# Two-layer encoder trunk on one core: the last down-projection block of the second tokens in two 256-column pieces at the mixers, and the first tokens' transposes in two parts

## The chip, the cores and the metric

The kernel runs on one core of one Trainium2 chip. The metric is device time in microseconds of one execution; lower is better. A core has five engines with a queue each: TensorE (PE in the rows; its weight loads are PEld), VectorE (DVE), ScalarE (ACT), GpSimd (POOL) and SyncE (SP, which issues DMAs). TensorE's results land in the banks of PSUM, from which VectorE and ScalarE read them.

## The reference

An encoder of two layers over 256 tokens of 1024 features, all in float32. Each layer is an FFN, a mixer and a second FFN, each with a residual, and a last norm follows:

```python
x = x + FFN_RES * swiglu(rms_norm(x, ffn1_norm[l]), ffn1_w_gate[l], ffn1_w_up[l], ffn1_w_down[l])
h = rms_norm(x, mix_norm[l])
proj = h @ w_in[l]
...
y = jnp.concatenate([rms_norm(y_rec, lru_out_norm[l]), rms_norm(y_att, attn_out_norm[l])], axis=-1)
x = x + y @ w_out[l]
x = x + FFN_RES * swiglu(rms_norm(x, ffn2_norm[l]), ffn2_w_gate[l], ffn2_w_up[l], ffn2_w_down[l])
```

with `rms_norm(x, g) = x * rsqrt(mean(x*x) + eps) * g`, `swiglu = (silu(x @ w_gate) * (x @ w_up)) @ w_down`, and D_FF = 2816. The mixer has a recurrent group of eight blocks (convolution, gates, a scan in both directions) and a windowed attention with eight heads.

## The kernel before, in words

**Precision.** Every float32 matmul is made of three: the weights are split into `wh` and `wl`, the activations into `xh` and `xl` (or `hh` and `hl`), and `wh*xh + wl*xh + wh*xl` is summed in PSUM. ScalarE writes the high part as a copy with rounding (L303 for weights, L540 for x), VectorE the low part as a difference (L304, L542).

**Stages.** There are six: FFN, mixer, FFN, twice. x stays in SBUF as two tiles of 128 tokens x 1024, "first tokens" (t = 0) and "second tokens" (t = 1). An FFN's hidden width is 22 blocks of 128 (NM = 22). Its body computes gate and up of a block and, some blocks later, adds the block's share of the down projection to four accumulators in PSUM: two banks `ps_a` for the first tokens, two banks `ps_b` for the second, 512 columns each. The last four blocks (TAIL = 4) are left to `tail`, which the boundary calls.

**The boundary** (`boundary`, L588 to L623) joins a stage to the next. It finishes the down projection for the first tokens (`tail(0, 0)`), adds each half to x (`evac`, L792), takes the sums of squares on ScalarE (`squares`, L510), rstd (a sum on VectorE, L497, a power on POOL, L500), and the norm in four pieces of 256 columns (L517). Meanwhile TensorE does most of the second tokens' tail: `tail(1, 1)`, four blocks for the first half of the columns and three (CUT = 3) for the second. Then come eight transposes of the first tokens (`transposes(0)`, L535, into `ps_a`), the last block of the second half (`tail(1, 2)`: three matmuls of 128x512, L581 to L583), `head(0)`, eight transposes of the second tokens (into `ps_b`) and `head(1)`. In a mixer, `head` is `natural` (L543 to L552): 24 matmuls of 128x256, k = 0 to 7 three times (`xh*wh`, `xh*wl`, `xl*wh`), with the weights `w_w` for k 0 to 3 and `w_i` for k 4 to 7. In an FFN it is 24 matmuls of 128x512 (L697). Boundaries 1 and 4 lead into mixers (`gi % 3 == 1`), 2, 3 and 5 into FFNs.

**Buffers.** `xn_p` has one buffer: the tile `xn` (128x1024) holds the squares, which nobody reads, then the norm, and goes from the first tokens to the second and into the next stage. Banks `ps_g` and `ps_c` are taken in turn by `bank("gc")`.

**What sets the order.** TensorE, SP and POOL run in the order of the program. ScalarE and VectorE are ordered at build time by a scheduler, which takes what is inside `front()` first; the order is then fixed, and each engine works its queue off in that order. `prefetch` splits weights ahead (L303 and L304), at a boundary behind the instructions in `state["behind"]`.

Of the kernel before, what the change touches and what calls it, by code (L numbers as in the profile page):

```python
# [32 lines left out]
TAIL = 4  # L33
# [8 lines left out]
MAHEAD = 5  # L42
# [13 lines left out]
CUT = 3  # L56
# [11 lines left out]
def encoder_kernel(  # L68
# [313 lines left out]
    def setup_early():  # L382
        idle = ep_p.tile([128, T], F32R, tag="th", name="idle")
        dve.memset(idle.bitcast(F32), 0.0)
        pi = bank("b")

        def keep_warm(n):
            for _ in range(n):
                pe.matmul(pi[:, 0:T], idle[:, 0:128], idle, start=True, stop=True)

        dve.memset(half_t, -0.5)
        dve.memset(ones_t, 1.0)
        load_x(0)
        rows8 = xn_p.tile([128, DM], F32, tag="xn", name="rows8")[0:KD, 0:128]
        nc.scalar.dma_start(out=rows8, in_=ffn1_norm[0].rearrange("(k c) -> k c", c=128))
        nc.scalar.dma_start(out=eye_t, in_=eye)
        ps = bank("b")
        keep_warm(WARM)
        pe.transpose(ps[:, 0:KD], rows8, eye_t[0:KD, 0:KD])
        keep_warm(WARM2)  # L400
        dve.tensor_copy(out=gcol, in_=ps[:, 0:KD])
# [7 lines left out]

    def first_norm(t):  # L410
        r = rstd_of(ss_t[t], 2)
        xn = xn_t[t] = xn_p.tile([128, DM], F32, tag="xn", name="xn")
        for c in range(0, DM, 256):
            dve.tensor_scalar(xn[:, c:c + 256], xt[t][:, c:c + 256], r, None, ALU.mult)

    def first_transposes(t):
        if t == 0:
            new_x()
        for hf in range(2):
            ps = bank("ab"[t])  # L420
            for j in range(4):
                k = hf * 4 + j
                xT[t, k] = ps[:, j * 128:(j + 1) * 128]
                pe.transpose(xT[t, k], xn_t[t][:, k * 128:(k + 1) * 128], eye_t)

    def first_split(lo, t, k):
        ts_, g = slice(t * 128, (t + 1) * 128), gcol[:, k:k + 1]
# [74 lines left out]

    ss_t = {}

    def squares(t, hf):
        if hf == 0:
            ss_t[t] = st_p.tile([128, 2], F32, tag="ss", name="ss")
            xn_t[t] = xn_p.tile([128, DM], F32, tag="xn", name="xn")
        sl = slice(hf * 512, hf * 512 + 512)
        return act.activation(out=xn_t[t][:, sl], in_=xt[t][:, sl], func=AF.Square,  # L510
                              scale=1.0 / math.sqrt(DM), accum_out=ss_t[t][:, hf:hf + 1])

    def norm(t, gi):
        r = rstd_of(ss_t[t], 2)
        for c in range(0, DM, 256):
            sl = slice(c, c + 256)
            ins = dve.scalar_tensor_tensor(out=xn_t[t][:, sl], in0=xt[t][:, sl], scalar=r, in1=gain_t[gi][:, sl],  # L517
                                           op0=ALU.mult, op1=ALU.mult)
        return ins

# [1 line left out]
        cur["x"] = x_p.tile([128, 2, KD, T], F32R, tag="xhl", name="xhl")  # L522
        cur["h"], cur["l"] = cur["x"][:, 0], cur["x"][:, 1]

    def transposes(t):
        if t == 0:
            new_x()
        xn = xn_t.pop(t)
        ts_ = slice(t * 128, (t + 1) * 128)
        parts = []  # L530
        for hf in range(2):
            ps = bank("ab"[t])
            for j in range(4):
                k = hf * 4 + j
                pe.transpose(ps[:, j * 128:(j + 1) * 128], xn[:, k * 128:(k + 1) * 128], eye_t)  # L535
# [49 lines left out]
    def front():  # L585
        return tc.high_priority(offset=FRONT)

    def boundary(tail, evac, gi, head, ahead):  # L588
        prefetch(ahead)
        state["cap"] = ahead  # L590
        state["ahead"] = AHEAD
        tail(0, 0)
        with front():
            for hf in range(2):
                evac(0, hf)
                squares(0, hf)
            norm(0, gi)
        tail(1, 1)
        with front():
            evac(1, 0)  # L600
            transposes(0)
            squares(1, 0)
        tail(1, 2)
        with front():
            evac(1, 1)
            i1 = squares(1, 1)
            i2 = norm(1, gi)
        prefetch(ahead)
# [73 lines left out]
    def ffn(st, acc_done):  # L682
# [78 lines left out]
        def dn(m, t, hfs, fin):  # L761
            if t not in acc:
                acc[t] = [bank("ab"[t]) for _ in range(2)]
            hh, hl = hh_t[m]
            for hf in hfs:
                end = NM - TAIL if st == (DEPTH - 1, 2) and (t, hf) == (1, 1) else NM
                stream(acc[t], hh, hl, W(st, "d", m), t, (hf,), m == 0, m == end - 1)
            if fin:
                done((st, "d", m))
                del hh_t[m]  # L770

        def tail(t, part):
# [50 lines left out]

        if st == (DEPTH - 1, 2):
            tail, evac = dn_cols, acc
        return head if st != (0, 0) else first_head, body, tail, evac

    def mix(l):
        st = (l, 1)
# [157 lines left out]
        def att_pt(i):  # L987
            pr = stat.pop(i)
            if "pt" not in late:
                late["pt"] = xn_p.tile([128, 2, 512], F32, tag="xn", name="pt")  # L990
            for e in range(2):
                ps = bank("b")
                for kb in range(2):
                    for b in range(2):
                        c = kb * T + b * 128
                        pe.transpose(ps[:, c:c + 128], pr[:, e, b, kb * 128:(kb + 1) * 128], eye_t)
                pt = late["pt"][:, e, :]
                act.activation(out=pt, in_=ps, func=AF.Copy)

        def att_pv(i):  # L1000
            if not po:
                for b in range(2):
                    po[b] = bank("a")
            for e in range(2):
                h = i + 4 * e
                pt = late["pt"][:, e, :]
# [13 lines left out]
        def att_norm(t):  # L1020
            if "o" not in late:
                late["o"] = mix_p.tile([128, 2, 512], F32, tag="ql", name="o")
            o = late["o"][:, t, :]
            dve.tensor_tensor(out=o.rearrange("p (h d) -> p h d", h=NH),
                              in0=po[t].rearrange("p (h d) -> p h d", h=NH),
                              in1=nm_t[:, :, t:t + 1].to_broadcast([128, NH, 64]), op=ALU.mult)
            ss = st_p.tile([128, 2], F32, tag="ss", name="ss")
            act.activation(out=late["pt"][:, t, :], in_=o, func=AF.Square, scale=1.0 / math.sqrt(LW), accum_out=ss[:, 0:1])
            ra[t] = rstd_of(ss, 1)

        def o_split(t):
# [93 lines left out]
                if n == "D":  # L1125
                    load_gain(3 * l + 2)

        return head, body, tail, evac

    engines = mybir.EngineType  # L1130
    with tc.manual_schedule(engines={engines.PE, engines.SP, engines.Pool}):
# [16 lines left out]
        state["behind"] = []  # L1148
        load_gain(1)
        for s in range(3 * DEPTH):  # L1150
            _, body, tail, evac = stages[s]
            body()
            n = s + 1
            if n == 3 * DEPTH:
# [52 lines left out]
```

## Time and profile before

| | us |
|---|---|
| median of 3 runs | 940.01 (939.6 to 940.08) |
| profiled execution | 940.3 |
| its span | 938.5 |
| TensorE busy | 925.9 (99% of the span) |
| VectorE busy | 696.5 (74%) |
| ScalarE busy | 544.7 (58%) |
| POOL busy | 37.0 (4%) |

The profiled execution is one run with the profiler on; its span goes from the first instruction to the last, and 1.8 us lie around it. Matmuls overlap: a row's duration is from start to the end of its result, and the next matmul starts before that end. So the time that a matmul takes on TensorE is read from the distance of two starts. "x8" in a row is a run of eight instructions, with the time from the first's start to the last's end. "[0.44 <-DVE xn L517]" is idle time before the row and what ended it.

### The profile page before, as it was taken

What the parts mean: (1) busy time and instruction counts of PE and PEld (TensorE: products, weight loads), DVE (VectorE), ACT (ScalarE), POOL (GpSimd) and SP (SyncE); (2) the same over time, 40 slices, a digit from 0 to 9 for tenths busy, and PEclk for the clock granted to TensorE, in tenths of its full rate; (3) what the DMA queues carried; (4) which work ended last, traced back from release to release, by engine and by line L of the source; (5) the groups of instructions that cost most, each with busy time, mean ns of one, the idle gap of its engine ahead of it and who ended that gap; (6) DMA issues with size and microseconds to landing.
All of it is one profiled execution on the core that took longest, in us unless ns stands there. A gap on an engine that the chain in (4) does not pass through costs nothing.

```text
span 938.5 us, 13682 instructions
## 1 busy us (share of the span) xinstructions
PE 925.9 (99%) x5288; PEld 804.8 (86%) x5288; DVE 696.5 (74%) x1212; ACT 544.7 (58%) x1006; POOL 37.0 (4%) x58
## 2 busy tenths in 40 slices
PE   8999999999999999999999999999999999999997
PEld 7888888889988888888888888888999888888885
DVE  6877666759998866666688666666799887666663
ACT  7755555547865655555466555554687565555542
POOL 4100000000010000000030000000000100000000
PEclk9999999999999999999999999999999999999999
DMA  8966955614255866565557565655162566665521
GB/s 279 304 211 200 326 192 183 228 64 154 91 157 179 262 197 191 179 192 196 175 174 252 181 186 198 199 179 179 49 223 68 180 233 203 197 196 182 184 86 45
DMA packets 124993, 172.54 MB, mean 184 GB/s; under 512 B 3920, under 2 KB 108792, under 8 KB 124928
## 3 DMA queue, kind: packets, MB, share of 16 engines
q1 hardware_dynamic: 122192, 166.21, 54.7%
q0 software_dynamic: 2288, 4.87, 1.6%
q8 instruction: 41, 0.67, 0.3%
q10 hardware_dynamic: 448, 0.59, 0.2%
q14 instruction: 24, 0.20, 0.1%
HBM read 170.59 MB, written 3.16 MB: 185 GB/s over the span
## 4 chain that ended last, share of the span: by engine, by line
PE 92%; ACT 2%; DVE 2%; DMA 1%; issue 1%; POOL 0%; POOLq 0%; DVEq 0%; ACTq 0%
PE ps_g L572 16%; PE ps_c L572 15%; PE ps_g L571 7%; PE ps_c L571 7%; PE ps_a L581 5%; PE ps_a L583 4%; PE ps_a L582 4%; PE ps_b L582 4%; PE ps_b L583 4%; PE ps_b L581 4%; PE ps_g L697 2%; PE ps_c L697 2%; PE ps_a L1010 1%; PE ps_g L561 1%; PE ps_g L560 1%; PE ps_g L562 1%
## 5 line engine op out<-in xcount | busy, mean ns | idle before, releaser
L304 DVE TENSOR_TENSOR wl<-raw,wh 128x1024 fp32r<-128x1024 f32 (+1 forms) x320 | 367.4, 1157 | 106.3 <-ACT wh L303 101.9
L303 ACT ACTIVATE wh<-raw 128x1024 fp32r<-128x1024 f32 (+1 forms) x306 | 301.6, 1000 | 89.0 <-PE ps_b L583 61.8
L572 PE MATMUL ps_g<-xhl,wh 128*128 128x512 f32 x640 | 231.5, 396 | 1.5 <-DVE hl L746 1.5
L572 PE MATMUL ps_c<-xhl,wh 128*128 128x512 f32 x640 | 231.2, 396 | 0.0
L571 PE MATMUL ps_g<-xhl,wl 128*128 128x256 f32 x560 | 156.5, 279 | 0.0
L571 PE MATMUL ps_c<-xhl,wl 128*128 128x256 f32 x560 | 156.2, 279 | 0.0
L572 PEld LDWEIGHTS ps_g<-xhl,wh 128*128 128x128 f32 x640 | 120.3, 188 | 24.6 <-issue 1.7
L572 PEld LDWEIGHTS ps_c<-xhl,wh 128*128 128x128 f32 x640 | 120.2, 188 | 22.8
L571 PEld LDWEIGHTS ps_g<-xhl,wl 128*128 128x128 f32 x560 | 105.6, 189 | 3.5
L571 PEld LDWEIGHTS ps_c<-xhl,wl 128*128 128x128 f32 x560 | 105.5, 188 | 3.5
L581 PE MATMUL ps_a<-wh,hh 128*128 128x512 f32 x168 | 65.8, 392 | 0.0
L581 PE MATMUL ps_b<-wh,hh 128*128 128x512 f32 x168 | 65.7, 391 | 0.0
L583 PE MATMUL ps_b<-wh,hl 128*128 128x512 f32 x168 | 65.4, 389 | 0.0
L582 PE MATMUL ps_b<-wl,hh 128*128 128x512 f32 x168 | 65.4, 389 | 0.0
L583 PE MATMUL ps_a<-wh,hl 128*128 128x512 f32 x168 | 65.4, 389 | 0.0
L582 PE MATMUL ps_a<-wl,hh 128*128 128x512 f32 x168 | 65.4, 389 | 0.0
L757 ACT ACTIVATE sg<-ps_g 128x256 f32<-128x256 f32 x40 | 15.4, 385 | 63.5 <-PE ps_g L572 63.5
L757 ACT ACTIVATE sg<-ps_c 128x256 f32<-128x256 f32 x40 | 15.3, 383 | 55.3 <-PE ps_c L572 54.6
L758 DVE TENSOR_TENSOR sg<-ps_g,sg 128x256 f32<-128x256 f32 x40 | 17.0, 425 | 32.1 <-ACT sg L757 32.1
L757 ACT ACTIVATE su<-ps_c 128x256 f32<-128x256 f32 x40 | 15.3, 382 | 38.7 <-PE ps_c L572 38.7
L582 PEld LDWEIGHTS ps_a<-wl,hh 128*128 128x128 f32 x168 | 31.6, 188 | 6.9
L583 PEld LDWEIGHTS ps_a<-wh,hl 128*128 128x128 f32 x168 | 31.5, 188 | 6.9
(320 smaller groups left out, 1579.2 us busy)
## 6 DMA issues: line engine op xcount, KB each, us to landing
raw<-in_ffn_w_down_dram SPq DMA_DIRECT2D x44, 1024.0 KB, 5.0
raw<-in_ffn_w_gate_dram SPq DMA_DIRECT2D x43, 1024.0 KB, 5.4
raw<-in_ffn_w_up_dram SPq DMA_DIRECT2D x43, 1024.0 KB, 5.4
raw<-in_w_in_dram SPq DMA_DIRECT2D x14, 1024.0 KB, 5.4
raw<-in_w_out_dram SPq DMA_DIRECT2D x8, 1024.0 KB, 7.3
lb<-ld POOLq DMA_DIRECT2D x1, 2048.0 KB, 14.8
bias_t<-lb POOLq DMA_DIRECT2D x1, 1536.0 KB, 12.5
gain<-in_ffn_norm_dram SPq DMA_DIRECT2D x3, 512.0 KB, 4.3
```

The lines of the kernel that those rows point to most:

```text
L303: act.activation(out=h3, in_=src, func=AF.Copy)
L304: dve.tensor_sub(out=l3, in0=src, in1=h3.bitcast(F32))
L560: pe.matmul(dst, wh[:, ks], xh[:, k, t0:t1], start=(k == 0), stop=False)
L561: pe.matmul(dst, wh[:, ks], xl[:, k, t0:t1], start=False, stop=False)
L571: pe.matmul(dst[:, 0:T], wl[:, ks], x2[:, 0, k, :], start=False, stop=False)
L572: pe.matmul(dst, wh[:, ks], x2[:, :, k, :], start=(k == 0), stop=(k == KD - 1))
L581: pe.matmul(acc[hf], ah[:, ts_], wh[:, cs], start=first, stop=False)
L582: pe.matmul(acc[hf], ah[:, ts_], wl[:, cs], start=False, stop=False)
L583: pe.matmul(acc[hf], al[:, ts_], wh[:, cs], start=False, stop=last)
L697: pe.matmul(ps, x, w[k // 2][p % 2][:, k % 2 * 512:k % 2 * 512 + 512], start=(p == 0 and k == 0), stop=(p == 2 and k == KD - 1))
L757: act.activation(out=s, in_=ps[:, T:2 * T], func=AF.Copy)
L758: dve.tensor_tensor(out=s, in0=ps[:, 0:T], in1=s, op=ALU.add)
```

## The change

In the boundaries into mixers, the last block's share of the second tokens' second half no longer goes into the accumulator `ps_b` as 512 columns. It goes into a bank of its own from the turn of `ps_g` and `ps_c`, as two pieces of 256 columns (`last(0)`, `last(1)`), and each piece is added to x by an instruction of its own (`add_last`). The accumulator itself is added to x a block earlier. The squares of that half are taken in two pieces too; a small sum joins them. At all five boundaries the eight transposes of the first tokens are parted into four and four, with the last block between them. `xn` becomes two tiles of 512 columns, `xn0` and `xn1`, with one buffer each; the mixer's `pt` and the start use the same tiles. The tile of sums goes from two columns to four.

```diff
+    def xn_half(hf, name="xn"):
+        return xn_p.tile([128, 512], F32, tag=f"xn{hf}", name=name)
...
-    def squares(t, hf):
+    def squares(t, hf, c=0, w=512):
         if hf == 0:
-            ss_t[t] = st_p.tile([128, 2], F32, tag="ss", name="ss")
-            xn_t[t] = xn_p.tile([128, DM], F32, tag="xn", name="xn")
-        sl = slice(hf * 512, hf * 512 + 512)
-        return act.activation(out=xn_t[t][:, sl], in_=xt[t][:, sl], func=AF.Square,
-                              scale=1.0 / math.sqrt(DM), accum_out=ss_t[t][:, hf:hf + 1])
-
-    def norm(t, gi):
-        r = rstd_of(ss_t[t], 2)
+            ss_t[t] = st_p.tile([128, 4], F32, tag="rr", name="ss")
+            xn_t[t] = []
+        if not c:
+            xn_t[t].append(xn_half(hf))
+        sl = slice(hf * 512 + c, hf * 512 + c + w)
+        j = hf + (c > 0)
+        ins = act.activation(out=xn_t[t][hf][:, c:c + w], in_=xt[t][:, sl], func=AF.Square,
+                             scale=1.0 / math.sqrt(DM), accum_out=ss_t[t][:, j:j + 1])
+        if hf and not c and w < 512:
+            dve.tensor_scalar(ss_t[t][:, 0:1], ss_t[t][:, 0:1], ss_t[t][:, 1:2], None, ALU.add)
+        return ins
+
+    def norm(t, gi, j=0):
+        r = rstd_of(ss_t[t][:, j:j + 2] if not j else ss_t[t][:, 0:3:2], 2)
...
-    def transposes(t):
-        if t == 0:
+    def transposes(t, hfs=(0, 1)):
+        if t == 0 and 0 in hfs:
             new_x()
...
-        for hf in range(2):
+        for hf in hfs:
...
-    def boundary(tail, evac, gi, head, ahead):
+    def boundary(tail, evac, gi, head, ahead, extra):
...
         with front():
             evac(1, 0)
-            transposes(0)
+            transposes(0, (0,))
             squares(1, 0)
-        tail(1, 2)
-        with front():
-            evac(1, 1)
-            i1 = squares(1, 1)
-            i2 = norm(1, gi)
+        if gi % 3 == 1:
+            last, add_last = extra
+            with front():
+                evac(1, 1)
+            last(0)
+            with front():
+                add_last(0)
+                squares(1, 1, 0, 256)
+            last(1)
+            with front():
+                add_last(1)
+                i1 = squares(1, 1, 256, 256)
+                transposes(0, (1,))
+                i2 = norm(1, gi, 1)
+        else:
+            tail(1, 2)
+            with front():
+                evac(1, 1)
+                transposes(0, (1,))
+                i1 = squares(1, 1)
+                i2 = norm(1, gi)
...
-                end = NM - TAIL if st == (DEPTH - 1, 2) and (t, hf) == (1, 1) else NM
+                end = NM
+                if (t, hf) == (1, 1):
+                    end -= TAIL if st == (DEPTH - 1, 2) else TAIL - CUT if st[1] == 0 else 0
...
+        def last(q):
+
+            if not q:
+                acc["own"] = bank("gc")
+            dn_cols(acc["own"][:, q * 256:q * 256 + 256], NM - 1, 1, 512 + q * 256, 768 + q * 256, True, q == 1)
+
+        def add_last(q):
+            sl = slice(512 + q * 256, 768 + q * 256)
+            dve.scalar_tensor_tensor(out=xt[1][:, sl], in0=acc["own"][:, q * 256:q * 256 + 256], scalar=0.25,
+                                     in1=xt[1][:, sl], op0=ALU.mult, op1=ALU.add)
```

How it moves the instructions at the first mixer boundary is shown for three engines, of before and then of the change. In the names, the number behind a tile tells its buffers apart; "waits" names whose semaphore an instruction waits for. First TensorE, from the last two transposes of the first tokens into the beginning of head(0):

```order
L535 MATMUL ps_a_2078<-eye_t_111,xn_2039 128x128 [waits DVE_49]
L535 MATMUL ps_a_2078<-eye_t_111,xn_2039 128x128
L581 MATMUL ps_b_697<-wh_1977,hh_1931 128x512
L582 MATMUL ps_b_697<-wl_1978,hh_1931 128x512
L583 MATMUL ps_b_697<-wh_1977,hl_1932 128x512
L552 MATMUL ps_c_2110<-w_w_1983,xhl_2072 128x256 [waits Activation_49]
L552 MATMUL ps_c_2110<-w_w_1983,xhl_2072 128x256
L552 MATMUL ps_c_2110<-w_w_1983,xhl_2072 128x256 [waits Activation_49]
L552 MATMUL ps_c_2110<-w_w_1983,xhl_2072 128x256
L552 MATMUL ps_c_2110<-w_i_1986,xhl_2072 128x256 [waits Activation_49]
```

```order
L823 MATMUL ps_c_2089<-wl_1980,hh_1933 128x256
L824 MATMUL ps_c_2089<-wh_1979,hl_1934 128x256
L822 MATMUL ps_c_2089<-wh_1979,hh_1933 128x256 [waits DVE_49]
L823 MATMUL ps_c_2089<-wl_1980,hh_1933 128x256
L824 MATMUL ps_c_2089<-wh_1979,hl_1934 128x256
L544 MATMUL ps_a_2102<-eye_t_111,xn_2044 128x128 [waits Activation_49]
L544 MATMUL ps_a_2102<-eye_t_111,xn_2044 128x128 x3
L561 MATMUL ps_g_2122<-w_w_1985,xhl_2075 128x256 [waits Activation_49]
L561 MATMUL ps_g_2122<-w_w_1985,xhl_2075 128x256
L561 MATMUL ps_g_2122<-w_w_1985,xhl_2075 128x256 [waits Activation_49]
L561 MATMUL ps_g_2122<-w_w_1985,xhl_2075 128x256
L561 MATMUL ps_g_2122<-w_i_1988,xhl_2075 128x256 [waits Activation_49]
```

The change's rows begin behind the first matmul of the first piece. The eight transposes are parted; the three 128x512 matmuls into `ps_b_697` became twice three of 128x256 into `ps_c_2089`, and the second L822 waits for VectorE (`add_last(0)`, which reads the other columns of that bank). Then four transposes into `ps_a_2102` and head(0), whose L561 with `w_i` (k 4) waits for ScalarE's copy of the second four.

Next ScalarE, from the copies of the first tokens' transposes (L540 before, L549 now) to those of the second tokens; L510, now L517, are squares:

```order
L540 ACTIVATE xhl_2072<-ps_a_2073 128x2x128 [waits PE_49]
L540 ACTIVATE xhl_2072<-ps_a_2073 128x2x128
L540 ACTIVATE xhl_2072<-ps_a_2078 128x2x128 [waits PE_49]
L540 ACTIVATE xhl_2072<-ps_a_2078 128x2x128
L510 ACTIVATE xn_2092,ss_2091<-x1_116 128x512 [waits DVE_49,Activation_49]
L510 ACTIVATE xn_2092,ss_2091<-x1_116 128x512 [waits DVE_49]
L303 ACTIVATE wh_2106<-raw_1999 128x1024 [waits DMAHW2_49]
L540 ACTIVATE xhl_2072<-ps_b_2135 128x2x128 [waits PE_49]
```

```order
L549 ACTIVATE xhl_2075<-ps_a_2076 128x2x128 [waits PE_49]
L549 ACTIVATE xhl_2075<-ps_a_2076 128x2x128
L517 ACTIVATE xn_2086,ss_2085<-x1_116 128x512 [waits DVE_49,Activation_49]
L517 ACTIVATE xn_2094,ss_2085<-x1_116 128x256 [waits DVE_49,PE_49,Activation_49]
L517 ACTIVATE xn_2094,ss_2085<-x1_116 128x256 [waits DVE_49]
L303 ACTIVATE wh_2118<-raw_2001 128x1024 [waits DMAHW2_49]
L549 ACTIVATE xhl_2075<-ps_a_2102 128x2x128 x2
L549 ACTIVATE xhl_2075<-ps_b_2147 128x2x128 [waits PE_49]
```

The copies from the second bank (`ps_a_2078`, now `ps_a_2102`) stood with the first ones, ahead of the squares; now they stand behind three squares and L303. The second of these squares waits for `add_last(0)` and, on PE, for the second four transposes, which read the tile that it writes. The copies of the second four wait for nothing else (the PE wait is met before them).

And VectorE, from the add of the second tokens' first half to x (L792, now L830) to rstd's sum:

```order
L792 SCALAR_TENSOR_TENSOR x_116<-ps_b,x_116 128x512 [waits PE_49]
L542 TENSOR_TENSOR xhl<-ps_a,xhl 128x2x128 [waits PE_49,Activation_49]
L542 TENSOR_TENSOR xhl<-ps_a,xhl 128x2x128
L792 SCALAR_TENSOR_TENSOR x_116<-ps_b,x_116 128x512 [waits PE_49]
L542 TENSOR_TENSOR xhl<-ps_a,xhl 128x2x128 [waits Activation_49]
L542 TENSOR_TENSOR xhl<-ps_a,xhl 128x2x128
L497 TENSOR_SCALAR rstd<-ss 128x1 [waits Activation_49]
```

```order
L830 SCALAR_TENSOR_TENSOR x_116<-ps_b,x_116 128x512 [waits PE_49] x2
L815 SCALAR_TENSOR_TENSOR x_116<-ps_c,x_116 128x256 [waits DVE_49,PE_49]
L551 TENSOR_TENSOR xhl<-ps_a,xhl 128x2x128 [waits Activation_49]
L551 TENSOR_TENSOR xhl<-ps_a,xhl 128x2x128
L815 SCALAR_TENSOR_TENSOR x_116<-ps_c,x_116 128x256 [waits PE_49]
L520 TENSOR_SCALAR ss<-ss 128x1 [waits Activation_49]
L501 TENSOR_SCALAR rstd<-ss 128x1 [waits DVE_49,Activation_49]
L527 SCALAR_TENSOR_TENSOR xn<-x_116,rstd,gain 128x256 [waits Pool_49]
```

Both halves of the accumulator are now added at once, then the first piece (L815), the low parts of k 0 to 3 (L551, L542 before), the second piece, the small sum (L520) and rstd's sum. The low parts of k 4 to 7, here before rstd's sum, are now further down, between the third and fourth piece of the norm.

At the second mixer boundary the three queues change alike. At boundaries into FFNs TensorE has four transposes, three matmuls of 128x512 and four transposes; ScalarE has the copies of k 0 to 3, `squares(1, 0)`, the copies of k 4 to 7, `squares(1, 1)`, then L303. From the first mixer's head to the second's the banks `ps_c` and `ps_g` have changed places, so that two output-projection groups of the first mixer meet other readers.

## Rows read from the trace of the kernel before

**Rows 1.** the page: busy us (share) x instructions of each engine; its chain by engine

```profile
PE 925.9 (99%) x5288; PEld 804.8 (86%) x5288; DVE 696.5 (74%) x1212; ACT 544.7 (58%) x1006; POOL 37.0 (4%) x58
PE 92%; ACT 2%; DVE 2%; DMA 1%; issue 1%; POOL 0%; POOLq 0%; DVEq 0%; ACTq 0%
```

**Rows 2.** TensorE's waits: total us, times, longest us

```profile
PE ps_b L535 <- DVE xn L517: 0.9, 2, 0.4
```

**Rows 3.** TensorE's timeline, first mixer boundary: start, us, what, [idle before]

```profile
198.15 1.03 PE L535 MATMUL ps_a<-eye_t,xn 128*128 128x128 f32 x8
198.94 0.48 PE L581 MATMUL ps_b<-wh,hh 128*128 128x512 f32 x1
199.26 0.39 PE L582 MATMUL ps_b<-wl,hh 128*128 128x512 f32 x1
...
199.72 0.64 PE L552 MATMUL ps_c<-w_w,xhl 128*128 128x256 f32 x4
...
202.06 0.63 PE L552 MATMUL ps_c<-w_i,xhl 128*128 128x256 f32 x4
203.13 1.54 PE L535 MATMUL ps_b<-eye_t,xn 128*128 128x128 f32 x8 [0.44 <-DVE xn L517]
204.43 0.71 PE L552 MATMUL ps_c<-w_w,xhl 128*128 128x256 f32 x4
...
207.64 0.28 PE L560 MATMUL ps_g<-xhl,wh 128*128 128x256 f32 x1
```

**Rows 4.** the same at the second mixer boundary: first and last of the stretch

```profile
656.96 1.03 PE L535 MATMUL ps_a<-eye_t,xn 128*128 128x128 f32 x8
...
666.44 0.28 PE L560 MATMUL ps_g<-xhl,wh 128*128 128x256 f32 x1
```

**Rows 5.** ScalarE's timeline at the first mixer boundary

```profile
198.79 1.21 ACT L540 ACTIVATE xhl<-ps_a 128x256 fp32r<-128x256 f32 x4 [3.75 <-PE ps_a L535]
...
200.87 0.63 ACT L510 ACTIVATE xn<-x 128x512 f32<-128x512 f32 x1 [0.26 <-DVE x L792]
...
201.50 1.04 ACT L303 ACTIVATE wh<-raw 128x1024 fp32r<-128x1024 f32 x1
203.92 1.45 ACT L540 ACTIVATE xhl<-ps_b 128x256 fp32r<-128x256 f32 x4 [1.38 <-PE ps_b L535]
```

**Rows 6.** VectorE's timeline at the first mixer boundary

```profile
197.57 0.68 DVE L792 SCALAR_TENSOR_TENSOR x<-ps_b,x 128x512 f32<-128x512 f32 x1
...
201.62 0.21 DVE L497 TENSOR_SCALAR rstd<-ss 128x1 f32<-128x1 f32 x1
202.50 1.67 DVE L517 SCALAR_TENSOR_TENSOR xn<-x,rstd,gain 128x256 f32<-128x256 f32 x4 [0.67 <-POOL rstd L500]
```

**Rows 7.** groups by form (busy us, mean ns | idle before): nearest operations

```profile
L758 DVE TENSOR_TENSOR sg<-ps_g,sg 128x256 f32<-128x256 f32 x40 | 17.0, 425 | 32.1 <-ACT sg L757 32.1
...
L979 ACT ACTIVATE pr<-pr,stn 128x256 f32<-128x256 f32 x32 | 15.8, 496 | 0.9 <-DVE stn L977 0.9
L540 ACT ACTIVATE xhl<-ps_a 128x256 fp32r<-128x256 f32 x20 | 6.1, 390 | 18.6 <-PE ps_a L535 18.6
L979 ACT ACTIVATION_READ_ACCUMULATOR pr<-pr,stn 128x1 f32 x32 | 6.0, 187 | 0.0
```

**Rows 8.** timeline at the boundary into the second layer's first FFN

```profile
471.79 1.03 PE L535 MATMUL ps_a<-eye_t,xn 128*128 128x128 f32 x8
...
472.42 1.21 ACT L540 ACTIVATE xhl<-ps_a 128x256 fp32r<-128x256 f32 x4 [3.75 <-PE ps_a L535]
```

**Rows 9.** timeline in the first mixer's output projection, TensorE and VectorE

```profile
264.67 0.39 PE L581 MATMUL ps_c<-wh,yh 128*128 128x512 f32 x1
...
264.51 0.42 DVE L932 SCALAR_TENSOR_TENSOR ge<-x,ps_g 128x256 f32<-128x256 f32 x1
```

**Rows 10.** windows: length, busy PE, PEld, DVE, ACT, POOL, granted clock, DMA, GB/s

```profile
10.00:14.00 4.00, 2.76 (x20) 2.08 (x18) 2.88 (x9) 3.60 (x10) 1.63 (x3) 1.00 1.09 353
195.00:203.00 8.00, 7.69 (x50) 6.76 (x48) 5.21 (x14) 3.52 (x10) 1.12 (x2) 1.00 0.00 0
```

More of the change, by code (lines that the diff above doesn't have):

```diff
@@ L393, in setup_early @@
         load_x(0)
-        rows8 = xn_p.tile([128, DM], F32, tag="xn", name="rows8")[0:KD, 0:128]
+        rows8 = xn_half(0, "rows8")[0:KD, 0:128]
         nc.scalar.dma_start(out=rows8, in_=ffn1_norm[0].rearrange("(k c) -> k c", c=128))
@@ L411, in first_norm @@
         r = rstd_of(ss_t[t], 2)
-        xn = xn_t[t] = xn_p.tile([128, DM], F32, tag="xn", name="xn")
+        xn_t[t] = [xn_half(hf) for hf in range(2)]
         for c in range(0, DM, 256):
-            dve.tensor_scalar(xn[:, c:c + 256], xt[t][:, c:c + 256], r, None, ALU.mult)
+            dve.tensor_scalar(xn_t[t][c // 512][:, c % 512:c % 512 + 256], xt[t][:, c:c + 256], r, None, ALU.mult)
     def first_transposes(t):
@@ L423, in first_transposes @@
                 xT[t, k] = ps[:, j * 128:(j + 1) * 128]
-                pe.transpose(xT[t, k], xn_t[t][:, k * 128:(k + 1) * 128], eye_t)
+                pe.transpose(xT[t, k], xn_t[t][hf][:, j * 128:(j + 1) * 128], eye_t)
     def first_split(lo, t, k):
@@ L503, in encoder_kernel @@
     ss_t = {}
-    def squares(t, hf):
+    def squares(t, hf, c=0, w=512):
         if hf == 0:
-            ss_t[t] = st_p.tile([128, 2], F32, tag="ss", name="ss")
-            xn_t[t] = xn_p.tile([128, DM], F32, tag="xn", name="xn")
-        sl = slice(hf * 512, hf * 512 + 512)
-        return act.activation(out=xn_t[t][:, sl], in_=xt[t][:, sl], func=AF.Square,
-                              scale=1.0 / math.sqrt(DM), accum_out=ss_t[t][:, hf:hf + 1])
-    def norm(t, gi):
-        r = rstd_of(ss_t[t], 2)
+            ss_t[t] = st_p.tile([128, 4], F32, tag="rr", name="ss")
[11 more added lines that the diff above has]
+        r = rstd_of(ss_t[t][:, j:j + 2] if not j else ss_t[t][:, 0:3:2], 2)
         for c in range(0, DM, 256):
             sl = slice(c, c + 256)
-            ins = dve.scalar_tensor_tensor(out=xn_t[t][:, sl], in0=xt[t][:, sl], scalar=r, in1=gain_t[gi][:, sl],
+            ins = dve.scalar_tensor_tensor(out=xn_t[t][c // 512][:, c % 512:c % 512 + 256], in0=xt[t][:, sl], scalar=r, in1=gain_t[gi][:, sl],
                                            op0=ALU.mult, op1=ALU.mult)
@@ L523, in new_x @@
         cur["h"], cur["l"] = cur["x"][:, 0], cur["x"][:, 1]
-    def transposes(t):
-        if t == 0:
+    def transposes(t, hfs=(0, 1)):
+        if t == 0 and 0 in hfs:
             new_x()
-        xn = xn_t.pop(t)
         ts_ = slice(t * 128, (t + 1) * 128)
         parts = []
-        for hf in range(2):
+        for hf in hfs:
             ps = bank("ab"[t])
@@ L534, in transposes @@
                 k = hf * 4 + j
-                pe.transpose(ps[:, j * 128:(j + 1) * 128], xn[:, k * 128:(k + 1) * 128], eye_t)
+                pe.transpose(ps[:, j * 128:(j + 1) * 128], xn_t[t][hf][:, j * 128:(j + 1) * 128], eye_t)
                 if j % 2:
@@ L825, in ffn @@
             tail, evac = dn_cols, acc
-        return head if st != (0, 0) else first_head, body, tail, evac
+        return head if st != (0, 0) else first_head, body, tail, evac, (last, add_last)
     def mix(l):
@@ L989, in att_pt @@
             if "pt" not in late:
-                late["pt"] = xn_p.tile([128, 2, 512], F32, tag="xn", name="pt")
+                late["pt"] = [xn_half(e, "pt") for e in range(2)]
             for e in range(2):
@@ L996, in att_pt @@
                         pe.transpose(ps[:, c:c + 128], pr[:, e, b, kb * 128:(kb + 1) * 128], eye_t)
-                pt = late["pt"][:, e, :]
+                pt = late["pt"][e]
                 act.activation(out=pt, in_=ps, func=AF.Copy)
@@ L1005, in att_pv @@
                 h = i + 4 * e
-                pt = late["pt"][:, e, :]
+                pt = late["pt"][e]
                 for b in range(2):
@@ L1027, in att_norm @@
             ss = st_p.tile([128, 2], F32, tag="ss", name="ss")
-            act.activation(out=late["pt"][:, t, :], in_=o, func=AF.Square, scale=1.0 / math.sqrt(LW), accum_out=ss[:, 0:1])
+            act.activation(out=late["pt"][t], in_=o, func=AF.Square, scale=1.0 / math.sqrt(LW), accum_out=ss[:, 0:1])
             ra[t] = rstd_of(ss, 1)
@@ L1126, in body @@
                     load_gain(3 * l + 2)
-        return head, body, tail, evac
+        return head, body, tail, evac, None
     engines = mybir.EngineType
@@ L1150, in encoder_kernel @@
         for s in range(3 * DEPTH):
-            _, body, tail, evac = stages[s]
+            _, body, tail, evac, extra = stages[s]
             body()
@@ L1159, in encoder_kernel @@
             first = index[(n // 3, n % 3), "kv", 0] if n % 3 == 1 else index[(n // 3, n % 3), "gu", 0]
-            boundary(tail, evac, n, stages[n][0], first + (MAHEAD if n % 3 == 1 else 3))
+            boundary(tail, evac, n, stages[n][0], first + (MAHEAD if n % 3 == 1 else 3), extra)
 _INS = ['x', 'ffn1_norm', 'ffn1_w_gate', 'ffn1_w_up', 'ffn1_w_down', 'mix_norm', 'w_in', 'conv_w', 'conv_b',
```

## The prediction

> **What bounds the kernel now.** I read the page's busy times and chain first. TensorE is busy for 925.9 of 938.5 us and holds 92% of the chain [rows 1]: whatever puts an idle stretch, or an instruction more, on TensorE's queue between two stages lengthens the run by that much, and work of the other engines counts only where TensorE waits for it. Then the table of TensorE's waits: at the two boundaries into the mixers it waits 0.9 us in all, for the norm of the second tokens [rows 2]. That is all that a better boundary could take from a wait.
>
> Then the timeline of TensorE at the first of these boundaries [rows 3]. From the first transpose of the first tokens (198.15) to the first q/k/v matmul behind both heads (207.64) there are 9.49 us. The work in them: 16 transposes at 0.10 us (eight take 198.15 to 198.94), three 128x512 matmuls at 0.23, 48 matmuls of 128x256 at 0.117 (twenty take 199.72 to 202.06), and 0.09 us whenever matmuls follow transposes (198.94 to 199.26 is 0.32 instead of 0.23). That makes some 8.1 us; the other 1.4 is waiting: before and inside the second tokens' transposes, and in the first eight matmuls of head(1), which follow the copies. The second mixer has the same stretch, 656.96 to 666.44 [rows 4], so one working serves for both.
>
> ScalarE's timeline shows what feeds TensorE there [rows 5]: four copies of the transposes (198.79 to 200.00, the next one 0.27 after the last), the second tokens' squares, then an L303 weight split of 1.04 us, then the copies for head(1). VectorE adds the two halves to x (0.68 us each, from 197.57) and takes rstd's sum at 201.62 [rows 6].
>
> **The change, part by part.**
>
> *The order of TensorE at the mixers.* Four transposes (k 0 to 3) to 198.55. First piece: three matmuls of 128x256 from 198.55, TensorE free at 198.99, results complete at 198.87 + 0.28 = 199.15. The second piece lies in the same bank and waits for VectorE's add of the first: VectorE has the other half's add behind it at 199.04 (0.68 from 198.36), begins at 199.19, and takes 0.42 us, which is what the nearest 128x256 operation from PSUM costs [rows 7]. So it ends at 199.61. TensorE follows VectorE by 0.15 us (the norm's first piece ends 0.48 after 202.50, the transposes start at 203.13 [rows 3, 6]): second piece at 199.77, **a new stall of 0.78 us**. The bank turns up in the order as a wait for the VectorE instruction that reads the other columns. The Trainium skill ("PSUM — Partial Sum Buffer", "PSUM bank collisions raise a hardware error") says that PSUM is to be guarded by bank and quadrant, not by address; by that rule this wait is necessary, and a guard by address would take 0.7 us per mixer off the sum. The sum follows the order.
>
> *The copies of k 4 to 7.* The second piece ends at 200.13, the other four transposes at 200.53, head(0) takes k 0 to 3 and stands at k 4 at 201.09. In ScalarE's order the copies of k 4 to 7 stand behind three things. Both halves of squares(1,1) come first; the first of them waits for the transposes too, as xn1 has one buffer. A copy began 0.64 us after its first transpose [rows 3, 5], so this is 200.77. Squares of 128x256 are not in this trace; the nearest, a 128x256 activation with an accumulator, takes 0.496 and 0.187 for the read, about 0.49 apart [rows 7]. A plain 128x256 copy at 0.39 is the lower bound, the 128x512 squares at 0.63 the upper [rows 5, 7]; I take 0.49 as the same shape and kind. Then L303 from 201.76 to 202.80, and the first copy from 202.71 to 203.10 (neighbours overlap by 0.1). TensorE follows at 203.23, as it follows the copies for head(1) by 0.12 (203.92 + 0.39, 204.43 [rows 3, 5]): **a second stall of 2.14 us**, of which L303 is half.
>
> *What comes back.* Head(0) has 20 matmuls left and ends at 205.58. The second sum of squares is complete at 201.85, where before rstd's sum could begin at 201.62 already, so the pieces don't bring the norm forward. With one small sum more, the 0.88 from rstd's sum to the first piece (201.62 to 202.50 [rows 6]) and the late copies' subtractions between them, four pieces end near 205.2, ahead of the transposes' need. So the second transposes need no wait. Copies from 206.22, head(1) from 206.73, eight matmuls at the copies' pace 0.27 per pair of k (1.05), sixteen at 0.117: 209.66. Behind its transposes head(1) takes 4.08 instead of 4.51, and the 0.44 before them is gone; that is within the 209.66. **Sum per mixer: 209.66 - 207.64 = +2.0 us.** Bounds: +1.2 if the second piece needn't wait, +2.7 with the squares at 0.63 each and nothing recovered in head(1).
>
> *The boundaries into the three FFN stages.* Here the last block keeps its 512 columns and only four transposes move behind it. TensorE changes kind once more: 3 x 0.09 = 0.27 us. The copies of k 4 to 7 come behind squares(1,0) but ahead of L303. From the order's sequence on this boundary's clock [rows 8]: transposes to 472.19 and 472.96 to 473.36; ScalarE copies to 473.0, squares to 473.7, the first late copy to 474.1; TensorE needs k 4 after four 128x512 matmuls, at 474.35. Hidden, with 0.25 us in hand; if that goes, up to 0.3 each.
>
> *Banks.* The bank of its own turns the parity of the c/g banks from the first mixer to the second. In the first mixer the output projection's second half (264.67) now waits for the VectorE read of a gate that runs from 264.51 to 264.93 [rows 9]: 0 to 0.47 us, I take 0.3. The squares' tag, the xn tiles in halves, the DMA queues and POOL keep their places and cost nothing: they add no instruction, and the queues' orders are the same.
>
> **Total:** 2 x 2.0 + 0.27 + 0.3 = +4.6 us. The profiled execution took 940.3, with 938.5 in the span, so it would become 944.9; the median of the runs shown is 0.3 lower, so **944.6**.
>
> **Rivals.** *A: the second piece isn't held.* If the add of the first is done before TensorE asks, or costs it little, each mixer is 0.7 shorter: 943.2. Against it: TensorE has nothing between the two pieces. 0.14.
>
> *B: not slower, because ScalarE serves the late copies first.* The place is L303 and the two squares in ScalarE's queue. If the copies went straight behind their transposes, at 200.77, k 4 would wait 0.2 instead of 2.14; the squares would come 0.6 later and the norm's wait return. A mixer would cost about +0.5, the whole 1.6 with FFN and banks: 941.6, which is within 0.2% (1.9 us, about what a measurement of this kernel can tell from no change). It decides at 1 us: with L303 behind the copies, half of this is already reached. Against it: the build fixes the order, and in [rows 5] ScalarE's starts follow it. 0.05.
>
> *C: the clock falls.* Between 198.99 and 203.23 TensorE would now work for only some 1.3 us. The granted clock is 1.00, the 2.4 GHz level, in this stretch and also at the start, where TensorE is busy for 2.76 of 4 us [rows 10]; no row shows 1.2 GHz. At that level the 4 us behind the stall would take 4 more at each mixer: 953. The Trainium skill ("TensorE: Matmul & The Clock Gate", "HAM oscillation — how this bites in real kernels") describes TensorE gated down after waits between groups of matmuls; by that page this would be a danger of such a boundary, but the stretch from 10 to 14 us speaks against it. 0.04.
>
> *D: the mixers' own queues.* ScalarE and VectorE are reordered a little within the mixers (weight splits against the scan's activations), and start 2 us later against the DMAs. The places I followed keep 0.7 us in hand, so no cost; if one turns into a wait, 1 to 2 us: 945.6 to 946.6, or the other way by as much. 0.14, of which 0.02 faster, 0.01 the same.
>
> **How the numbers follow.** The forecast keeps 0.63. The range takes in the bounds of the sum (2 x 1.2 at the low end with nothing else: 942.4; 2 x 2.7 + 0.6 + 0.5, 946.5), A whole, and most of D: 942.2 to 947.4. Outside are B, C and a small part of D, some 0.12, with about 0.06 for the mis-sized forecast. Slower: 0.63 + 0.14 + 0.04 + 0.11 = 0.92; same: B and a hundredth of D, 0.06; faster: 0.02.
>
> **What would show it.** In the changed profile: TensorE's wait table with about 0.8 us at each mixer for the VectorE add in the matmul of the second piece, and about 2.1 each in head(0) for a ScalarE copy; the 0.9 us of the norm gone; 9.5 us of the stretch grown to 11.5; ScalarE's L303 between squares and copies. The forecast is wrong if the stalls are there but the stretch is below 10.5 (head(1) recovered more), or if the stretch fits and the time doesn't (then the mixers took or gave the rest).

## The result, and the profile after

The changed kernel takes 949.46 us (median of 5 runs, 948.15 to 949.9) against 940.01: a ratio of 1.0096, 95% interval 1.0084 to 1.0107. The forecast was 944.6 with a range of 942.2 to 947.4: the side was right, the size about half. The profiled execution took 949.9 us with a span of 948.1, so 9.6 us are to be found against the span of before.

The page's busy times (here and below, a number in brackets names the rows of before to compare with) [rows 1]:

```profile
PE 930.0 (98%) x5294; PEld 807.9 (85%) x5294; DVE 698.1 (74%) x1218; ACT 546.0 (58%) x1010; POOL 37.0 (4%) x58
```

TensorE has 4.1 us more of "busy", though only a few instructions more: the first sign that the same work ran slower somewhere. TensorE's waits [rows 2]:

```profile
PE ps_g L561 <- ACT xhl L549: 1.8, 1, 1.8
PE ps_c L561 <- ACT xhl L549: 1.8, 1, 1.8
...
PE ps_g L822 <- DVE x L815: 0.5, 1, 0.5
PE ps_c L822 <- DVE x L815: 0.5, 1, 0.5
PE ps_g L569 <- DVE ge L970: 0.5, 1, 0.5
PE ps_c L569 <- DVE ge L970: 0.5, 1, 0.5
...
PE ps_c L569 <- DVE xc L918: 0.2, 1, 0.2
PE ps_g L569 <- ACT i_t L947: 0.2, 1, 0.2
```

The first four are the two forecast stalls, once at each mixer boundary. (Idle time counts from the end of the last result; between starts the two stalls are 2.0 and 0.67 us.) The norm's wait is gone. L569 is a projection inside the mixer: these waits are new (there is one of each at either mixer), and the forecast put them at nothing, with a chance of 0.14 for its rival D. TensorE's timeline at the first mixer boundary [rows 3], and the ends of the stretch at the second [rows 4]:

```profile
198.18 0.60 PE L544 MATMUL ps_a<-eye_t,xn 128*128 128x128 f32 x4
...
198.86 0.28 PE L824 MATMUL ps_c<-wh,hl 128*128 128x256 f32 x1
199.66 0.39 PE L822 MATMUL ps_c<-wh,hh 128*128 128x256 f32 x1 [0.52 <-DVE x L815]
...
200.12 0.60 PE L544 MATMUL ps_a<-eye_t,xn 128*128 128x128 f32 x4
200.47 0.72 PE L561 MATMUL ps_g<-w_w,xhl 128*128 128x256 f32 x4
202.98 1.22 PE L561 MATMUL ps_g<-w_i,xhl 128*128 128x256 f32 x4 [1.78 <-ACT xhl L549]
203.99 1.05 PE L561 MATMUL ps_g<-w_w,xhl 128*128 128x256 f32 x4
204.85 1.05 PE L561 MATMUL ps_g<-w_i,xhl 128*128 128x256 f32 x4
...
206.98 1.04 PE L544 MATMUL ps_b<-eye_t,xn 128*128 128x128 f32 x8
...
211.11 0.28 PE L569 MATMUL ps_c<-xhl,wh 128*128 128x256 f32 x1
...
661.87 0.60 PE L544 MATMUL ps_a<-eye_t,xn 128*128 128x128 f32 x4
...
674.82 0.28 PE L569 MATMUL ps_g<-xhl,wh 128*128 128x256 f32 x1
```

The stretch is 12.93 us at the first mixer, 12.95 at the second, where it was 9.49 and 9.48. Behind the stall four matmuls of 128x256 take 0.85 us (203.99 to 204.85); before, and again later, four take 0.47. The windows of this stretch (length; busy PE, PEld, DVE, ACT, POOL; granted clock; DMA) say why [rows 10]:

```profile
198.54:202.98 4.44, 2.14 (x18) 1.73 (x16) 2.82 (x8) 3.44 (x11) 0.55 (x1) 1.00 0.01 2
202.98:206.51 3.53, 3.53 (x17) 3.53 (x17) 3.12 (x7) 0.22 (x1) 0.00 (x0) 0.52 0.00 0
206.51:211.11 4.60, 4.56 (x39) 4.33 (x37) 2.65 (x5) 2.15 (x5) 0.00 (x0) 1.00 0.02 4
```

From the end of the stall TensorE is granted half its clock (the 1.2 GHz level), until about 206.4; then 2.4 GHz again. Head(0)'s last 20 matmuls take 4.00 us (202.98 to 206.98), where 20 x 0.117 would be 2.34 and the same 20 take 2.50 in e1 below, with the clock at 1.00: 1.5 us for the low clock. ScalarE's timeline is the one that was worked out [rows 5]: squares, L303, and only then the copies.

```profile
200.81 0.42 ACT L517 ACTIVATE xn<-x 128x256 f32<-128x256 f32 x1 [0.72 <-ACT xn L517]
...
201.22 0.40 ACT L517 ACTIVATE xn<-x 128x256 f32<-128x256 f32 x1
...
201.62 1.04 ACT L303 ACTIVATE wh<-raw 128x1024 fp32r<-128x1024 f32 x1
202.57 0.63 ACT L549 ACTIVATE xhl<-ps_a 128x256 fp32r<-128x256 f32 x2
```

**Where the 9.6 us are**, by starts of the same instruction in both traces: the mixer boundaries 3.44 and 3.47; the rest of the two mixers 1.37 and 1.17; the three FFN boundaries 0.04, 0.06 and 0.06. Within the first mixer TensorE falls back at three matmuls by 0.47, 0.12 and 0.59, at the waits for `i_t`, `xc` and `ge` above, and by 0.2 at the output projection.

The largest of the three shows the mechanism in VectorE's queue. Before, the gelu's last step `ge`, which reads the bank that TensorE needs next, stood between two scans:

```profile
252.70 0.68 DVE L922 TENSOR_TENSOR_SCAN i_t<-a_t,i_t 128x256 f32<-128x256 f32 x1
253.29 0.40 DVE L932 SCALAR_TENSOR_TENSOR ge<-x,ps_c 128x256 f32<-128x256 f32 x1
253.61 0.68 DVE L924 TENSOR_TENSOR_SCAN i_t<-a_t,i_t 128x256 f32<-128x256 f32 x1
```

Now it stands behind both, one scan (0.6 us) later, and the matmul that reuses its bank waits for it (last row); before, that matmul started at 253.74, with no idle time ahead of it:

```profile
256.76 0.68 DVE L960 TENSOR_TENSOR_SCAN i_t<-a_t,i_t 128x256 f32<-128x256 f32 x1
257.36 0.67 DVE L962 TENSOR_TENSOR_SCAN i_t<-a_t,i_t 128x256 f32<-128x256 f32 x1
257.94 0.40 DVE L970 SCALAR_TENSOR_TENSOR ge<-x,ps_g 128x256 f32<-128x256 f32 x1
258.40 0.39 PE L569 MATMUL ps_g<-xhl,wh 128*128 128x256 f32 x1 [0.51 <-DVE ge L970]
```

### The profile page after: what moved, and what is told of

The parts are those of the page before. It is cut to its first block, busy times and chain, and to the rows that moved or that the text cites. A ratio compares the mean times of both kernels' runs of the same rounds, so it can differ in the third digit from the quotient of the medians.

```text
span 948.1 us, 13707 instructions
## 1 busy us (share of the span) xinstructions
PE 930.0 (98%) x5294; PEld 807.9 (85%) x5294; DVE 698.1 (74%) x1218; ACT 546.0 (58%) x1010; POOL 37.0 (4%) x58
## 4 chain that ended last, share of the span: by engine, by line
PE 88%; DVE 5%; ACT 4%; issue 2%; DMA 1%; POOL 0%; POOLq 0%; DVEq 0%; ACTq 0%
PE ps_g L581 15%; PE ps_c L581 15%; PE ps_g L580 7%; PE ps_c L580 7%; PE ps_a L590 4%; PE ps_a L592 4%; PE ps_a L591 4%; PE ps_b L592 4%; PE ps_b L591 4%; PE ps_b L590 4%; PE ps_g L722 2%; PE ps_c L722 2%; PE ps_g L583 1%; PE ps_c L583 1%; DMA raw<-in_ffn_w_down_dram 1%
## 5 line engine op out<-in xcount | busy, mean ns | idle before, releaser
L303 ACT ACTIVATE wh<-raw 128x1024 fp32r<-128x1024 f32 (+1 forms) x306 | 302.0, 1000 | 91.8 <-PE ps_b L592 61.5
L590 PE MATMUL ps_a<-wh,hh 128*128 128x512 f32 x168 | 65.8, 392 | 0.0
L590 PE MATMUL ps_b<-wh,hh 128*128 128x512 f32 x166 | 64.7, 390 | 0.0
L783 DVE TENSOR_TENSOR sg<-ps_c,sg 128x256 f32<-128x256 f32 x40 | 16.9, 423 | 27.6 <-ACT sg L782 27.6
```

The lines of the kernel that those rows point to most:

```text
L303: act.activation(out=h3, in_=src, func=AF.Copy)
L590: pe.matmul(acc[hf], ah[:, ts_], wh[:, cs], start=first, stop=False)
L783: dve.tensor_tensor(out=s, in0=ps[:, 0:T], in1=s, op=ALU.add)
```

## The experiments

Theory: three costs, each with its own cause: the stalls from the queue order at the boundary; the clock from the stalls; the mixers' 1.2 us from the order that the scheduler gives VectorE and ScalarE inside the mixer. Rivals: the clock falls for another reason; the mixers wait because of the turned banks, the pieces, or because they start late. Each comparison below is with runs of the kernel before on the same chip (medians 940.25 to 940.41).

**e1: fill the stall.**

```diff
+        if gi % 3 == 1:
+            for _ in range(2):
+                ps = bank("b")
+                for j in range(8):
+                    pe.transpose(ps[:, j % 4 * 128:j % 4 * 128 + 128], eye_t, eye_t)
         head(0)
```

> The changed kernel, with 16 transposes of the unit matrix (some 1.6 us, nobody reads them) on TensorE between the second four transposes and head(0) at both mixer boundaries. ScalarE and VectorE keep the changed kernel's order at the boundary and in the mixers. Theory 1 (TensorE's waits at the boundary, 0.7 and 2.0 us, are why the granted clock falls to 0.50, and the low clock is worth 1.65 us a mixer): k 4 comes as late as before, but the clock stays at 1.00, so the time is 949.5 - 2 x 1.65 = 946.2 us; the three waits inside each mixer (1.2 us a mixer) stay. Rival (the clock falls for another reason, or costs nothing beside the wait): 949.5 us with two stretches at 0.50 as now.

Measured: 946.57 us, ratio 1.0069 (1.0054 to 1.0084). Windows of the same two stretches:

```profile
198.39:202.84 4.45, 3.88 (x34) 3.47 (x32) 2.84 (x8) 3.45 (x11) 0.56 (x1) 1.00 0.01 2
202.84:206.40 3.56, 3.53 (x28) 3.30 (x28) 3.12 (x7) 0.64 (x3) 0.00 (x0) 1.00 0.02 5
```

k 4 comes 4.45 us behind the first piece's start, as in the changed kernel (4.44), and 16 transposes more are done; head(0)'s last 20 matmuls end 2.50 us later (205.34), where they took 4.00; so the run is 2.9 us shorter (3.3 when each is compared with before on its own chip) with more work in it, since the clock stays at 1.00. The stretch is 11.42 and 11.40 instead of 12.93 and 12.95. The three waits in each mixer stay. TensorE's idling is the cause of the low clock, and a low clock is worth 1.5 us a mixer.

**e2: the copies first.**

```diff
             last(0)
             with front():
                 add_last(0)
-                squares(1, 1, 0, 256)
             last(1)
             with front():
+                transposes(0, (1,))
                 add_last(1)
+                squares(1, 1, 0, 256)
                 i1 = squares(1, 1, 256, 256)
-                transposes(0, (1,))
```

> The changed kernel with the copies of k 4 to 7 ahead of squares(1, 1) and of L303 in ScalarE's queue; the two pieces in one bank and its turn stay. Inside the mixers VectorE and ScalarE then stand in the order of the kernel before. Theory 1 (stall of k 4 by the queue, clock by the stall, 1.2 us a mixer by the order inside the mixers): k 4 waits 0.2 us, the clock stays at 1.00, a boundary costs about 0.5 (0.3 to 0.9) over before and the mixers nothing: 941.3 us (940.8 to 942.2). Rival (the mixers' waits come from the turn of the banks or from the pieces): 2.4 us more, 943.7.

Measured: 942.23 us, ratio 1.0021 (1.0012 to 1.003), just above the upper end of what was expected. Of TensorE's waits at the mixers only these are left:

```profile
PE ps_c L822 <- DVE x L815: 0.5, 1, 0.5
PE ps_g L822 <- DVE x L815: 0.5, 1, 0.5
PE ps_c L590 <- DVE ge L970: 0.2, 1, 0.2
```

The stretch is 10.27 and 10.25, 0.8 over before, with the clock at 1.00. The waits for `i_t`, `xc` and `ge` in L569 are gone, though pieces and turned banks are all there; the turn costs the 0.2 at the output projection (L590), once.

**e3: only L303 behind the copies.**

```diff
-                transposes(0, (1,))
+                i0 = transposes(0, (1,))[0]
...
-        state["behind"] = [i1, i2]
+        state["behind"] = [i0, i1, i2] if gi % 3 == 1 else [i1, i2]
```

> The changed kernel with only L303 moved behind the copies of k 4 to 7; both squares stay ahead of them. The mixers keep the changed order. The wait for k 4 is 1.0 instead of 2.0 us. If the clock falls all the same, the boundaries give back 0.95 each: 947.6 us. If the shorter wait leaves the clock at 1.00, they give back 2.6 each: 944.3 us. 1.2 us a mixer stay in both cases.

Measured: 945.01 us, ratio 1.0052 (1.0035 to 1.0068): the second case. The wait for k 4 is halved and the clock stays:

```profile
198.44:201.94 3.50, 2.15 (x18) 1.73 (x16) 2.48 (x7) 2.50 (x10) 0.00 (x0) 1.00 0.00 0
201.94:205.50 3.56, 3.52 (x29) 3.29 (x29) 2.96 (x7) 1.61 (x4) 0.56 (x1) 1.00 0.01 2
```

The stretch is 10.46 at both mixers. One instruction of 1.04 us in front of the copies cost 2.5 us a mixer: its own time and the clock.

**e4: the mixers' order without the change.** e1's 16 transposes, put ahead of head(0) in the kernel before; the order inside the mixers then turns as in the changed kernel.

> The kernel before, with 16 transposes of the unit matrix (1.6 us, nobody reads them) ahead of head(0) at both mixer boundaries: no pieces, no bank of its own, no parted transposes, no idle TensorE. The scheduler then orders VectorE and ScalarE inside the mixers as in the changed kernel (but for one place). Theory 1 (that order is worth 1.2 us a mixer): the boundary itself becomes 0.9 to 1.2 longer, as the wait for the norm goes, and 2 x (1.0 + 1.2) = 4.4 us come on top of before: 944.4 us, with the waits for i_t, xc and ge in TensorE's table. Rival (those waits came from the flipped banks, the pieces or the low clock): 942.0 us and none of these waits.

Measured: 944.79 us, ratio 1.0048 (1.0033 to 1.0063). The stretch is 10.55 at both mixers, 1.06 over before, and TensorE's table has the mixers' waits, two each:

```profile
PE ps_c L560 <- DVE ge L937: 1.0, 2, 0.5
...
PE ps_c L560 <- DVE xc L885: 0.5, 2, 0.3
PE ps_g L560 <- ACT i_t L914: 0.4, 2, 0.2
```

There is no piece, no turned bank, no parted transpose and no low clock in this kernel. 4.4 less 2 x 1.06 leaves 2.3 us, 1.15 a mixer, for the order.

**e5: a bank for each piece.**

```diff
-            if not q:
-                acc["own"] = bank("gc")
-            dn_cols(acc["own"][:, q * 256:q * 256 + 256], NM - 1, ...
+            acc["own", q] = bank("gc")
+            dn_cols(acc["own", q][:, q * 256:q * 256 + 256], NM - 1, ...
```

> The changed kernel with the two pieces in two banks, so that the second doesn't wait for the add of the first (the turn of the banks is then again that of before). ScalarE's queue stays: squares and L303 ahead of the copies of k 4 to 7; the mixers keep the changed order. The first wait (0.67 us at each mixer) goes, and everything behind it is 0.7 earlier; the wait for k 4 stays at 1.9 us. If that wait alone makes the clock fall: 949.5 - 1.4 = 948.1 us. If it took both waits together: 944.8 us with the clock at 1.00.

Measured: 946.78 us, ratio 1.0069 (1.0054 to 1.0084): between the two cases; in the profiled execution the clock did both. The windows of the profiled execution, from the first piece to k 4 and from there on, at the first and the second mixer:

```profile
198.28:201.93 3.65, 1.86 (x17) 1.66 (x14) 2.69 (x8) 3.37 (x11) 0.55 (x1) 1.00 0.01 2
660.82:664.47 3.65, 1.86 (x18) 1.65 (x15) 2.70 (x8) 3.37 (x11) 0.55 (x1) 1.00 0.01 2
201.93:205.50 3.57, 3.53 (x29) 3.30 (x29) 3.12 (x7) 0.67 (x3) 0.00 (x0) 1.00 0.00 0
664.47:668.49 4.02, 4.02 (x20) 4.02 (x21) 3.11 (x7) 0.21 (x1) 0.00 (x0) 0.58 0.00 0
```

TensorE did the same before both, and only behind the second did the clock fall; the stretches are 10.61 and 12.15. So the wait for the add is real and goes with a second bank (k 4 comes 3.65 us behind the first piece's start instead of 4.44), and the wait for k 4 alone may or may not bring the clock down. (The profiled execution, 947.67, also has one wait of 1.5 us in the first mixer, behind a weight that landed late.)

**e6: no pieces.** The mixers take the FFNs' branch: parted transposes, the last block as before.

```diff
-        if gi % 3 == 1:
-            last, add_last = extra
...
-        else:
+        if True:
...
-                    end -= TAIL if st == (DEPTH - 1, 2) else TAIL - CUT if st[1] == 0 else 0
+                    end -= TAIL if st == (DEPTH - 1, 2) else 0
```

> The transposes parted at all five boundaries, xn in two tiles, but no pieces and no bank of its own: at the mixers as at the FFNs. Inside the mixers the order of before. Theory: the parts of the change that are no pieces cost next to nothing: TensorE changes kind once more (0.05 to 0.09 us a boundary), k 4 waits 0.3 us at the mixers, and the norm of the second tokens comes 0.3 earlier: within 0.5 us of before. Rival (parting the transposes is what costs): more than 1 us over before.

Measured: 939.9 us, ratio 0.9996 (0.9986 to 1.0005): no difference. In its trace the mixer stretch is 9.27 us instead of 9.49, and the norm's wait is gone:

```profile
198.10 0.60 PE L544 MATMUL ps_a<-eye_t,xn 128*128 128x128 f32 x4
...
202.82 1.57 PE L544 MATMUL ps_b<-eye_t,xn 128*128 128x128 f32 x8
...
207.37 0.28 PE L569 MATMUL ps_g<-xhl,wh 128*128 128x256 f32 x1
```

Parting the transposes alone costs nothing here; the pieces bring the rest with them.

**e7: an attempt at a faster one.** e6 at the mixers only, and a head by halves of k:

```diff
-        for p in range(3):
-            for k in range(KD):
+        for p, k in [(p, k) for q in range(2) for p in range(3) for k in range(4 * q, 4 * q + 4)]:
+            for _ in range(1):
```

> The attempt at a version faster than both: transposes parted at the mixers alone, the last block in the accumulator as before, and the mixers' head takes k 0 to 3 for all three products, then k 4 to 7, so that the copies of k 4 to 7 have 1.4 us more. Inside the mixers the order of before. TensorE has no wait for k 4, the second transposes begin 0.3 us earlier: 0.3 to 0.5 us a mixer, 0.6 to 1.0 us below before, which three rounds may not tell from no change. If the low parts of x come too late for the third product of k 0 to 3, it is no gain or up to 0.5 us more.

Measured: 940.06 us, ratio 0.9997 (0.9987 to 1.0006): no difference. Head(0) has no stall, but head(1) waits for the low parts: k 0 to 3 take 1.94 us there (204.02 to 205.96) against 1.59 in head(0) (199.45 to 201.04), and the stretch takes 9.39:

```profile
204.02 2.11 PE L561 MATMUL ps_c<-w_w,xhl 128*128 128x256 f32 x12
205.96 1.56 PE L561 MATMUL ps_c<-w_i,xhl 128*128 128x256 f32 x12
```

**e8: the change, with the mixers' old order.**

```diff
-        for p in range(3):
-            for k in range(KD):
+        for p, k in [(p, k) for k in range(KD) for p in range(2)] + [(2, k) for k in range(KD)]:
+            for _ in range(1):
```

> The changed kernel whole, its queue order at the boundary too (squares and L303 ahead of the copies of k 4 to 7), but in the mixers' head TensorE takes both products of the high part for each k before the next k, so that 0.94 instead of 0.47 us of work lie ahead of k 4. Inside the mixers VectorE and ScalarE then stand in the order of before. Theory (1.2 us a mixer hang on that order and not on the boundary's lateness): none of the waits for i_t, xc and ge, 2.4 us less than the changed kernel. The wait for k 4 becomes 1.4 instead of 2.0, but k 4 comes at the same time, and 0.47 less follows behind it: 1.3 us a boundary over before without the clock. Sum with the clock at 1.00: 940.2 + 2.6 + 0.2 + 0.2 = 943.2 us; with a low clock at both mixers up to 946.5. Rival (the mixers wait because they start late): 945.6 or more, with those waits in the table.

Measured: 943.29 us, ratio 1.0033 (1.0021 to 1.0046). The waits of its table at the mixers:

```profile
PE ps_g L561 <- ACT xhl L549: 1.3, 1, 1.3
PE ps_c L561 <- ACT xhl L549: 1.3, 1, 1.3
...
PE ps_g L822 <- DVE x L815: 0.5, 1, 0.5
PE ps_c L822 <- DVE x L815: 0.5, 1, 0.5
```

Both stalls are there, the first stretch is 10.78, the clock stays at 1.00, and the mixers, which begin more than a microsecond late as in e4, have none of the three waits. e4 and e8 together show the order as the cause, not the lateness. The traces of all runs agree: up to the output projection VectorE and ScalarE work the mixers in one and the same new order in the changed kernel, e1, e3, e4 and e5, which all have these waits, and in the order of before in e2, e6, e7 and e8, which have none.

## Why the prediction was wrong

**The two stalls: right.** The second piece was forecast at 199.77 and came at 199.66 on a clock 0.03 later; k 4 at 203.23 and 202.98. The squares of 256 columns took 0.41 each from start to start, not the 0.49 taken from the nearest row (the lower bound was nearer). The second transposes needed no wait; behind them head(1) took 4.13 (206.98 to 211.11), forecast 4.08. Without the clock the boundary cost 3.44 - 1.5 = 1.9 us, forecast 2.0. The guard by bank held: the second piece waited for the add of the first (0.52 us idle), and e5 shows the wait gone with two banks. The Trainium skill's rule ("PSUM — Partial Sum Buffer", "PSUM bank collisions raise a hardware error") to guard by bank and not by address agrees with that order; what an unguarded second piece would do, no run here shows.

**Rival C came true beside the forecast; its 0.04 was the worst step.** I had the place (198.99 to 203.23) and the little work in it, and dismissed it by the start of the run, where TensorE works 2.76 of 4.00 us at the full clock. That row was of another kind: TensorE is busy for 2.14 of 4.44 us in this stretch, with two waits. A row that shows the clock up is no evidence for a stretch with less work. The forecast's "no row shows 1.2 GHz" was true of the rows it shows, not of the trace: at the end of before, after TensorE's last matmul (931.29), the clock does fall:

```profile
936.70:938.50 1.80, 0.00 (x0) 0.00 (x0) 0.00 (x0) 0.00 (x0) 0.00 (x0) 0.51 0.02 5
```

The price was too high instead: 4 us a mixer forecast, 1.5 measured, because the low level held for 3.4 us (203.0 to 206.4) and was over before head(0) ended. 2 x 1.5 = 3.0 us. The Trainium skill ("TensorE: Matmul & The Clock Gate", "HAM oscillation — how this bites in real kernels") describes a TensorE throttled after each long wait for a DMA between groups of matmuls. The trace agrees that the clock falls behind waits (0.52 granted from 202.98 to 206.51), but here behind two shorter ones, 0.52 and 1.78 us idle, with work between them. The forecast's signs of being wrong had none for a stretch longer than 11.5 us.

**Rival D came true too, as a certainty of the build.** The forecast said that the places I followed keep 0.7 us in hand. I had followed the chain of `xch` and `xcl` to the gate matmuls, and not the three places where a matmul reuses a bank that a reordered reader frees later. The orders of both programs were at hand, so this could be read: 1.18 us a mixer, 2.4 in all, a little more than the rival's 1 to 2 us in all. It is independent of the boundary, so forecast and rival added up; a list of cases of which one alone occurs was the wrong form.

**The small terms** were too large: FFN boundaries 0.16 of 0.27, the output projection's bank 0.2 of 0.3. In sum: 2 x 1.94 + 2 x 1.5 + 2 x 1.18 + 0.35 = 9.6 us.

**Rival B was sized nearly right, in part by luck:** with the copies first the whole was forecast at 941.6, e2 measured 942.23; a mixer boundary cost 0.8 instead of the forecast 0.5, and the smaller terms made up for part of it. **Rival A** needed the second bank: e5 took 0.8 us from the time to k 4, forecast 0.7.

## What to carry to other kernels

A stall of 2 us on a queue that was 99% busy is not only its own time: look whether the clock falls behind it, and give that a real chance whenever TensorE will do less in a stretch than in any stretch of the trace. Where a scheduler orders an engine at build time, a change in one place can reorder the next stage; compare the releaser of every reused bank there, not only the chain of operands. And costs with separate causes are added, not weighed against each other.

## What had not been expected of the hardware

The same work and the same wait (3.65 us with TensorE busy 1.86 of them) was followed by a clock of 1.00 at one mixer and by 0.5 at the other, in one execution of e5. With both waits, 2.14 of 4.44 us, it fell at both mixers in the profiled execution; with 2.61 of 4.44 (e8) and with 2.15 of 3.50 (e3) it stayed at both. What decides between two equal stretches stays open. It fits that the changed kernel's runs spread over 948.15 to 949.9, by about the price of one fall, while the five runs of before beside them lie within 0.5 us. The mean granted clock of each run goes with it: 0.994, 0.994 and 0.995 in the three longest (949.46 to 949.9, the profiled one with its two falls among them), 0.996 and 0.997 in the other two (948.15 and 948.62), where one fall of 3.4 us at half clock is 0.002 of such a mean. So the two shorter runs probably had one fall; they were not traced. In e1, e3 and e8 no run's mean is below 0.997.
